# Higher priority for norm and attention steps than for weight splits, and bias tables stored in 16 parts, in a decoder trunk on one core

## The chip, the cores and the metric

The kernel runs on one core of one Trainium2 chip. The metric is device time in microseconds (us); lower is better. The time before is the median of three runs, and one further execution was profiled.

## The reference, cut to what matters

The reference is a decoder trunk of four layers on 256 tokens of width 1024, all in float32. Each layer is a half-step feed-forward (FFN), a token mixer, and a second half-step FFN. Every part is normalised before and after, and added to the residual `x`.

```python
for i in range(DEPTH):                                  # DEPTH = 4
    x = x + 0.5 * rms_norm(swiglu(rms_norm(x, g[0]), w_in[i, 0], w_out[i, 0]), g[1])
    m = mixer[i % 3](rms_norm(x, g[2]))                 # 0: sliding window with sinks, 1: NSA, 2: MoBA
    x = x + rms_norm(m, g[3])
    x = x + 0.5 * rms_norm(swiglu(rms_norm(x, g[4]), w_in[i, 1], w_out[i, 1]), g[5])
```

The mixers have 16 heads of 64 and one bias table by distance, shared by all layers. Layers 0 and 3 use the sliding window of 128, layer 1 uses NSA (compressed blocks, selected blocks and a window), and layer 2 uses full causal blocks.

## The kernel before, in words

**Chains.** The 256 tokens are two tiles of 128, `t` = 0 and 1. Each tile is a chain of steps (`Chain.run`), written as a Python generator that yields the time at which its next step can start. A planner (`choose`, with a `Clock` that books an estimated time for each instruction) interleaves the two chains. The order of TensorE is exactly the order that the planner writes (`ORDERED`). On the other engines a scheduler at compile time orders the instructions: by its own estimate of when an instruction's inputs are there, and among those that are ready on an engine it takes the one with the lowest priority number, which is the place in the written order. At run time each engine takes its instructions in the order so fixed.

**Weights and their splits.** A float32 product is made of three products of a faster kind: a weight is split into `hi` and `lo`, an activation into `xh` and `xl`, and TensorE adds `hi*xh`, `lo*xh` and `hi*xl`. `feed` does the weights: a load of 512 KB (`raw<-wts`, queue SP, 4 buffers), a copy on ScalarE (`hi<-raw`), a subtraction on VectorE (`lo<-raw,hi`). It is called once at each step of the planner's loop, so splits are written ahead of the steps that come after them. Up to 28 slots (`k4`) hold split halves and the attention's tiles, and `room` says how many are left.

**The steps named in the change.**
- `boundary` ends a part: `var` squares the accumulators on ScalarE, `rsqrt` is on GpSimd, the residual `x` is updated on VectorE, then `split_T` transposes the new `x` on TensorE (`trx`) and makes `xh` on ScalarE and `xl` on VectorE. The next part's first products wait for these.
- `core` is the attention core, in jobs of four heads. Scores (`acc<-k,k` in the profile) go to two PSUM banks, VectorE adds the bias and takes the maximum (`k<-acc,bias`), then come the negated maximum (`nm`), the exponentials on ScalarE (`k<-k,nm`), transposes on TensorE (`trp`) copied out to `pT` by both engines, products with the values (`pv`), and the weighing on VectorE (`weigh`). A chain has 4 jobs in layers 0, 2 and 3, and 8 in layer 1.
- In layer 1 two more generators run beside the cores, `compress` and `cmp_core`. Their instructions on ScalarE and VectorE are not touched by the change.
- `setup` builds the bias tables once, early in layer 0: two products, two copies, and four stores to `scratch` in memory (`scratch<-k`), the planner letting `SGAP` = 8 us pass between them. `bias` loads a job's table from there in four parts (`bias<-scratch`).
- `project` multiplies the norm's output with a block of weights in two halves of the 1024 input rows (`proj`); the second half needs `xl[4]` and on.

All queue-SP transfers (weights, tables, biases, gains) are issued in one order. Because of a helper, nearly all instructions have line 210 (ScalarE, VectorE, GpSimd), 228 (products), 235 (transposes) or 248 (transfers) in the profile, so tiles tell them apart.

Of the kernel before, what the change touches and what calls it, by code (L numbers as in the profile page):

```python
# [10 lines left out]
F32 = mybir.dt.float32  # L11
# [32 lines left out]
PACE = 1.2  # L44
LATE = 6
SETUP = 30
SGAP = 8
SOON = 3
HALVES = (slice(0, DH), slice(DH, P))
FIRST, CMP_CORE = -1, 1.5  # L50
# [210 lines left out]
def trunk(ctx: ExitStack, tc: tile.TileContext, x, rel, gains, pre, sinks, pos, w1, w2, wts, hot,  # L261
# [72 lines left out]
    def setup():  # L334
        relx = const.tile([33, 2, H], F32, name="relx")
        hots = k4(3, [P, HALF])[:33, :2 * LT]
        nc.sync.dma_start(relx[0:32], rel)
        nc.vector.memset(relx[32:33], 1.0)
        nc.sync.dma_start(hots, hot)
        nc.sync.dma_start(cm, cmask)  # L340
        nc.sync.dma_start(bm, bmask)
        nc.sync.dma_start(post, pos)
        nc.sync.dma_start(w2s, w2)
        for a in range(2):
            nc.sync.dma_start(nsink[:, a, :], sinks[a:a + 1, :].broadcast_to([P, H]))
        yield when(hots, relx), False
        rows = k4(3, [P, HALF])[:H, :2 * LT].rearrange("p (a b) -> p a b", a=2)
        for i in range(2):
            p = bank([P, 512], "tab")
            nc.tensor.matmul(p[:H, :LT], relx[:, i, :], hots[:, i * LT:(i + 1) * LT],  # L350
                             start=True, stop=True)
            nc.vector.tensor_copy(rows[:, i, :], p[:H, :LT])
        nc.vector.tensor_scalar_mul(nsink, nsink, -1.0)
        for i in (1, 0):
            for c in range(0, REP, REP // 2):
                nc.sync.dma_start(scratch[i, :, c:c + REP // 2],
                                  rows[:, i, :].unsqueeze(1).broadcast_to([H, REP // 2, LT]))
                yield clock.now + SGAP, False
        drop(3, 2)
        plan.want[3] = 0  # L360
# [52 lines left out]
    class Chain:  # L413
# [72 lines left out]
        def boundary(self, acc, this, coef, last=False):  # L486


            t = self.t
            x_ = xt[t]  # L490
            g = self.gain(*this)
            cols = [slice(q * 512, (q + 1) * 512) for q in range(2)]
            r = self.rsqrt(self.var(acc, 1.0 / (coef * coef)))
            ys = []
            for c, a in zip(cols, acc):
                y = k2([P, 512])
                nc.vector.tensor_tensor(y, a, g[:, c], op=ALU.mult)
                ys.append(y)
            accs.extend(acc)
            for c, y in zip(cols, ys):  # L500
                nc.vector.scalar_tensor_tensor(x_[:, c], y, r, x_[:, c], op0=ALU.mult, op1=ALU.add)
                if last:
                    nc.sync.dma_start(out[t * P:(t + 1) * P, c], x_[:, c])
            if last:
                return
            yield max(when(x_), free_bank()), False
            i, k = this
            norm = 6 * i + k + 1
            self.split_T(x_, 0, norm)
            self.split_T(x_, 1, norm)  # L510
            self.v = self.var([x_[:, c] for c in cols], 1.0)
            if t:
                load_gains(((norm + 1) // 6, (norm + 1) % 6))
            yield when(self.xl[0]), True
# [14 lines left out]
        def project(self, n):  # L529
            p = bank([P, 512], "proj")  # L530
            if n > 256:
                self.proj(p, n, 0, 4)
                yield 0.0, True
                self.proj(p, n, 4, 8)
            else:
                self.proj(p, n, 0, 8)
            return p
# [130 lines left out]
        def core(self, o, branches, table, sink=None):  # L668
# [11 lines left out]
            for n in range(len(jobs) + 2):  # L680
                new = None
                if n < len(jobs):
                    h0, br = jobs[n]
                    key = branches[br][0]
                    b0 = h0 // hb * hb
                    if br == 0 and b0 == h0 and b0 + hb < H:
                        biases[b0 + hb] = self.bias(table, b0 + hb)
                    bias = biases[b0][:, h0 - b0:h0 - b0 + 4, :]
                    yield max(free(*sc_), when(self.qT, key(h0))), False
                    for e in range(2):  # L690
                        rows = slice(DH * e, DH * e + DH)
                        for j in range(2):
                            h = h0 + 2 * j + e
                            nc.tensor.matmul(sc[e][:, j, :], self.qT[rows, h // 2, :],
                                             key(h)[rows, :nk], start=True, stop=True)
                    s = k4(t, [P, 4, nk]) if t else k2([P, 4, nk])
                    mx = self.small("mx", 4)
                    for e in range(2):
                        for j in range(2):
                            k = 2 * j + e  # L700
                            nc.vector.tensor_tensor_reduce(
                                s[:, k, :], sc[e][:, j, :], bias[:, k, :], 1.0, -3e38, ALU.add,
                                ALU.max, accum_out=mx[:, k:k + 1])
                    new = (h0, br, s, mx)
                if turned is not None:
                    h0, br, pTs, coef = turned
                    yield max(when(*pTs), free_bank()), False
                    pv = bank([P, 4, DH], "pv")
                    for half in range(2):
                        for c in range(nb):  # L710
                            k, kb = 2 * half + c // (t + 1), c % (t + 1)
                            for q in HALVES:
                                nc.tensor.matmul(pv[q, k, :], pTs[half][:, c, q],
                                                 branches[br][1](h0 + k, kb), share=0.25,
                                                 start=kb == 0, stop=kb == t)
                    self.weigh(o[:, h0 * DH:(h0 + 4) * DH], pv, coef, br == 0)
                done = None
                if fresh is not None:
                    h0, br, s, den, at = fresh
                    pTs = []  # L720
                    for half in range(2):
                        yield max(at[half], free_bank()), False
                        p = bank([P, nb, P], "trp")
                        for c in range(nb):
                            k, kb = 2 * half + c // (t + 1), c % (t + 1)
                            nc.tensor.transpose(p[:, c, :], s[:, k, kb * P:(kb + 1) * P], ident)
                        pT = pp.tile([P, nb, P], F32, tag="pT", name="pT")
                        if half:
                            nc.vector.tensor_copy(pT, p)
                        else:  # L730
                            nc.scalar.activation(pT, p, AF.Copy)
                        pTs.append(pT)
                    if t:
                        drop(t)
                    coef = self.recip(den)
                    gate = branches[br][2]
                    if gate is not None:
                        nc.vector.tensor_tensor(coef, coef, gate[:, h0:h0 + 4], op=ALU.mult)
                    done = (h0, br, pTs, coef)
                    fresh = None  # L740
                if new is not None:
                    h0, br, s, mx = new
                    nm = self.small("nm", 4)
                    if sink is None:
                        nc.vector.tensor_scalar_mul(nm, mx, -1.0)
                    else:
                        ns = nsink[:, sink, h0:h0 + 4]
                        nc.vector.scalar_tensor_tensor(nm, mx, -1.0, ns, op0=ALU.mult, op1=ALU.min)
                    den = self.small("den", 4)
                    at = []  # L750
                    for k in range(4):
                        nc.scalar.activation(s[:, k, :], s[:, k, :], AF.Exp, bias=nm[:, k:k + 1],
                                             accum_out=den[:, k:k + 1])
                        if k % 2:
                            at.append(when(s))
                    if sink is not None:
                        es = self.small("es", 4)
                        nc.vector.tensor_sub(es, nm, ns)
                        nc.scalar.activation(es, es, AF.Exp)
                        nc.vector.tensor_add(den, den, es)  # L760
                    fresh = (h0, br, s, den, at)
                turned = done
            accs.extend(sc_)
# [360 lines left out]
```

## Time and profile before

| | |
|---|---|
| median of three runs | 1981.14 us (1978.83 to 1983.23) |
| profiled execution, its own time | 1981.12 us |
| its span in the profile | 1979.3 us |
| TensorE busy | 1938.0 us, 98% |
| VectorE busy | 1234.2 us, 62% |
| ScalarE busy | 1039.2 us, 53% |
| mean granted TensorE clock | 0.994 |

The span runs from the first to the last instruction; the time has 1.8 us more around it. A busy TensorE is one that has a product under way, so its busy share does not say that it runs at its best rate.

### The profile page before, as it was taken

The numbers are of one execution on the slowest core, as the hardware profiler recorded it, in microseconds if no ns is written. First come the engines' busy times: TensorE is split into PE (matmuls) and PEld (weight loads), VectorE is DVE, ScalarE is ACT, GpSimd is POOL, SyncE is SP. The second block draws the span as 40 slices with busy tenths as digits, with TensorE's granted clock in tenths as the row PEclk, the third lists the DMA queues.
The fourth block names the chain that finished last, engine by engine and source line by source line (L and its number), as shares of the span: only waits on it lengthen the run. The fifth ranks groups of instructions, "written<-read, shape, count | busy, mean of one in ns | idle before, by whom it ended". The sixth has DMA issues, their size and how long they took to land.

```text
span 1979.3 us, 27414 instructions
## 1 busy us (share of the span) xinstructions
PE 1938.0 (98%) x9978; PEld 1586.7 (80%) x9978; DVE 1234.2 (62%) x2267; ACT 1039.2 (53%) x1885; POOL 43.0 (2%) x62
## 2 busy tenths in 40 slices
PE   7999999999999998999999999999999999999998
PEld 6778878888888876788888888778888888878887
DVE  6566666556655648765576556566557655676554
ACT  6345655445544546554455455655445544665442
POOL 0000000000000000000000000000000000000000
PEclk9999999999999999999999999999999999999999
DMA  8758556555556454465556555655555555436551
GB/s 271 210 192 241 176 137 200 190 185 186 195 188 193 153 165 116 139 202 188 185 170 209 185 185 175 188 148 196 185 189 181 195 188 191 161 112 205 185 186 58
DMA packets 114131, 356.42 MB, mean 180 GB/s; under 512 B 12843, under 2 KB 30507, under 8 KB 113996
## 3 DMA queue, kind: packets, MB, share of 16 engines
q1 hardware_dynamic: 113996, 354.68, 55.4%
q8 instruction: 78, 1.28, 0.3%
q14 instruction: 57, 0.47, 0.1%
HBM read 352.01 MB, written 2.62 MB: 179 GB/s over the span
## 4 chain that ended last, share of the span: by engine, by line
PE 90%; ACT 3%; DVE 3%; DMA 2%; issue 1%; SPq 0%; POOL 0%; DVEq 0%; POOLq 0%; ACTq 0%
PE proj L228 56%; PE acc L228 29%; ACT k L210 2%; PE trh L235 2%; DVE k L210 2%; DMA raw<-wts 1%; PE trx L235 1%; DVE lo L210 1%; PE pv L228 1%; DMA bias<-scratch 1%; PE trp L235 1%; ACT hi L210 1%; DVE pT L210 0%; PE trq L235 0%; ACT xh L210 0%
## 5 line engine op out<-in xcount | busy, mean ns | idle before, releaser
L210 DVE TENSOR_TENSOR lo<-raw,hi 128x1024 fp32r<-128x1024 f32 x625 | 760.3, 1223 | 371.3 <-ACT hi L210 338.7
L210 ACT ACTIVATE hi<-raw 128x1024 fp32r<-128x1024 f32 x625 | 659.3, 1063 | 369.3 <-PE acc L228 187.5
L228 PE MATMUL proj<-hi,xh 128*128 128x512 f32 (+1 forms) x1696 | 673.9, 398 | 2.7 <-DVE xl L210 1.7
L228 PE MATMUL proj<-lo,xh 128*128 128x512 f32 (+1 forms) x1696 | 657.4, 389 | 0.8 <-DVE lo L210 0.8
L228 PE MATMUL proj<-hi,xl 128*128 128x512 f32 (+1 forms) x1696 | 448.6, 387 | 0.0
L228 PEld LDWEIGHTS proj<-hi,xh 128*128 128x128 f32 x1696 | 320.0, 189 | 64.0 <-ACT xh L210 2.8
L228 PEld LDWEIGHTS proj<-lo,xh 128*128 128x128 f32 x1696 | 320.4, 189 | 61.4 <-DVE lo L210 1.1
L228 PEld LDWEIGHTS proj<-hi,xl 128*128 128x128 f32 x1696 | 315.6, 188 | 67.3
L228 PE MATMUL acc<-hi,hh 128*128 128x512 f32 x704 | 223.7, 392 | 3.1 <-ACT hh L210 3.1
L228 PE MATMUL acc<-lo,hh 128*128 128x512 f32 x704 | 222.2, 389 | 0.0
L228 PE MATMUL acc<-hi,hl 128*128 128x512 f32 x704 | 191.3, 390 | 0.0
L210 ACT ACTIVATE h<-proj,rh 128x256 f32<-128x256 f32 x176 | 81.9, 465 | 182.3 <-PE proj L228 180.8
L210 ACT ACTIVATE hh<-trh 128x256 fp32r<-128x256 f32 x176 | 67.0, 380 | 180.8 <-PE trh L235 180.7
L228 PEld LDWEIGHTS acc<-hi,hh 128*128 128x128 f32 x704 | 130.9, 188 | 30.2 <-ACT hh L210 3.9
L228 PEld LDWEIGHTS acc<-hi,hl 128*128 128x128 f32 x704 | 132.1, 188 | 27.7
L228 PEld LDWEIGHTS acc<-lo,hh 128*128 128x128 f32 x704 | 132.1, 188 | 27.6
L210 DVE SCALAR_TENSOR_TENSOR h<-h,proj 128x256 f32<-128x256 f32 x176 | 73.6, 418 | 116.2 <-ACT h L210 116.1
L210 DVE TENSOR_TENSOR hl<-trh,hh 128x256 fp32r<-128x256 f32 x176 | 73.9, 420 | 113.2 <-ACT hh L210 113.1
L210 DVE SCALAR_TENSOR_TENSOR h<-proj,c,h 128x256 f32<-128x256 f32 x176 | 85.0, 483 | 5.1
L210 ACT ACTIVATE k<-k,nm 128x128 f32<-128x128 f32 (+1 forms) x160 | 70.7, 445 | 32.0 <-DVE nm L210 32.0
L210 POOL TENSOR_TENSOR r<-v,mhalf 128x1 f32<-128x1 f32 x48 | 36.0, 750 | 1818.4 <-DVE v L210 1818.4
L235 PE MATMUL trh<-ident,h 128*128 128x128 f32 x352 | 67.0, 272 | 0.0
(99 smaller groups left out, 1133.4 us busy)
## 6 DMA issues: line engine op xcount, KB each, us to landing
raw<-wts SPq DMA_DIRECT2D x624, 512.0 KB, 4.6
bias<-scratch SPq DMA_DIRECT2D x96, 128.0 KB, 4.6
g<-gains SPq DMA_DIRECT2D x12, 512.0 KB, 4.8
k<-w SPq DMA_DIRECT2D x8, 512.0 KB, 8.3
scratch<-k SPq DMA_DIRECT2D x4, 384.0 KB, 6.6
out<-x SPq DMA_DIRECT2D x4, 256.0 KB, 2.0
x<-x SPq DMA_DIRECT2D x2, 256.0 KB, 3.0
x<-x SPq DMA_DIRECT2D x1, 512.0 KB, 7.2
```

Of the source, the lines that this page charges most:

```text
L210: return call(out, *args, **kw)
L228: self.engine.matmul(out, lhs, rhs, **kw)
L235: self.engine.transpose(out, src, ident)
```

## The change

1. `SGAP` goes from 8 to 6, and each of the two tables is stored in 8 parts of 4 rows instead of 2 parts of 16: 16 stores instead of 4, of the same bytes in sum.
2. A new constant `AHEAD` = 100. Instructions written inside `tc.high_priority(AHEAD)` get a priority number lower by 100, so among ready instructions of an engine they go before whatever was written up to some 100 instructions earlier. It is put around the post-norm, the residual update, `split_T` and `var` of `boundary`; and in `core` around the bias and maximum, the weighing, the copies `pT`, and the exponentials with `nm` and the sink terms. TensorE's order is written by hand and stays as the planner writes it; `feed`, `out_proj`'s own `split_T`, `compress` and `cmp_core` keep their numbers.
3. `project` yields `when(self.xl[4])` instead of `0.0` between its halves, so that the planner gives the second half no earlier time than that of its input.

```diff
-SGAP = 8
+SGAP = 6
+AHEAD = 100
...
-            for c in range(0, REP, REP // 2):
-                nc.sync.dma_start(scratch[i, :, c:c + REP // 2],
-                                  rows[:, i, :].unsqueeze(1).broadcast_to([H, REP // 2, LT]))
+            for c in range(0, REP, 4):
+                nc.sync.dma_start(scratch[i, :, c:c + 4],
+                                  rows[:, i, :].unsqueeze(1).broadcast_to([H, 4, LT]))
                 yield clock.now + SGAP, False
...
+            with tc.high_priority(AHEAD):
                 r = self.rsqrt(self.var(acc, 1.0 / (coef * coef)))
...
+            with tc.high_priority(AHEAD):
                 self.split_T(x_, 0, norm)
                 self.split_T(x_, 1, norm)
                 self.v = self.var([x_[:, c] for c in cols], 1.0)
...
-                yield 0.0, True
+                yield when(self.xl[4]), True
...
+                    with tc.high_priority(AHEAD):
                         s = k4(t, [P, 4, nk]) if t else k2([P, 4, nk])
                         mx = self.small("mx", 4)
...
+                    with tc.high_priority(AHEAD):
                         self.weigh(o[:, h0 * DH:(h0 + 4) * DH], pv, coef, br == 0)
...
+                        with tc.high_priority(AHEAD):
                             pT = pp.tile([P, nb, P], F32, tag="pT", name="pT")
...
+                    with tc.high_priority(AHEAD):
                         nm = self.small("nm", 4)
```

## Rows read from the trace of the kernel before

**Rows 1.** The page's first part: busy time, share of the span, instructions.
```profile
PE 1938.0 (98%) x9978; PEld 1586.7 (80%) x9978; DVE 1234.2 (62%) x2267; ACT 1039.2 (53%) x1885; POOL 43.0 (2%) x62
```
**Rows 2.** Stretches: length; busy us of PE, PEld, DVE, ACT, POOL; PEclk; DMA.
```profile
100.00:105.00 5.00, 3.64 (x16) 2.46 (x14) 2.54 (x5) 2.76 (x4) 0.00 (x0) 1.00 0.00 0
...
225.00:255.00 30.00, 29.38 (x251) 22.68 (x250) 21.04 (x96) 22.94 (x81) 0.00 (x0) 1.00 0.59 166
255.00:275.00 20.00, 18.02 (x149) 14.96 (x149) 12.57 (x48) 10.51 (x33) 0.55 (x1) 0.96 0.59 127
275.00:660.00 385.00, 385.00 (x1778) 316.84 (x1777) 242.94 (x354) 197.20 (x303) 6.92 (x9) 1.00 0.58 189
...
725.00:803.00 78.00, 67.65 (x806) 51.58 (x805) 67.20 (x275) 47.70 (x165) 6.33 (x8) 0.98 0.45 139
...
1268.00:1313.00 45.00, 41.43 (x385) 33.02 (x385) 30.91 (x124) 32.16 (x102) 0.55 (x1) 1.00 0.55 150
...
1729.00:1773.00 44.00, 40.80 (x344) 31.92 (x342) 30.31 (x127) 28.10 (x96) 0.55 (x1) 0.92 0.38 109
```
**Rows 3.** The chain that ended last, 725 to 806 us: start, us, what.
```profile
732.39 3.50 DVE lo L210 x3
...
762.81 1.13 DVE lo L210
...
798.38 1.11 DVE lo L210
```
**Rows 4.** Timeline of TensorE, 728 to 742 us.
```profile
734.05 1.68 PE L228 MATMUL acc<-k,k 64*128 64x128 f32 x16
```
**Rows 5.** The same chain, 1270 to 1315 us.
```profile
1268.99 1.08 ACT hi L210
...
1271.23 0.59 DVE lo L210
```
**Rows 6.** The same chain, 1720 to 1775 us.
```profile
1733.37 1.23 DVE lo L210
...
1735.47 7.28 DMA bias<-scratch
```
**Rows 7.** Timeline, 264 to 276 us: idle time before it in brackets.
```profile
266.07 1.22 DVE L210 TENSOR_TENSOR lo<-raw,hi 128x1024 fp32r<-128x1024 f32 x1
...
268.14 0.15 DVE L210 SCALAR_TENSOR_TENSOR nm<-mx,nsink 128x4 f32<-128x4 f32 x1
...
273.61 1.94 PE L235 MATMUL trx<-ident,x 128*128 128x128 f32 x8 [1.98 <-DVE x L210]
```
**Rows 8.** Timeline of ScalarE, 75 to 108 us.
```profile
99.49 0.38 ACT L210 ACTIVATE hh<-trh 128x256 fp32r<-128x256 f32 x1 [5.19 <-PE trh L235]
...
102.61 3.89 ACT L210 ACTIVATE hi<-raw 128x1024 fp32r<-128x1024 f32 x4
```
**Rows 9.** The page's transfers: KB each, median us to landing.
```profile
scratch<-k SPq DMA_DIRECT2D x4, 384.0 KB, 6.6
```
**Rows 10.** Groups: count, busy us, mean ns, idle before and releaser.
```profile
L210 DVE TENSOR_TENSOR lo<-raw,hi 128x1024 fp32r<-128x1024 f32 x625 | 760.3, 1223 | 371.3 <-ACT hi L210 338.7 <-PE acc L228 7.6 <-ACT xh L210 2.2
```
**Rows 11.** Waits of TensorE: total us, times, longest.
```profile
PE proj L228 <- DVE xl L210: 1.7, 2, 1.3
PE proj L228 <- DVE lo L210: 0.8, 1, 0.8
```
**Rows 12.** Timelines of VectorE and of TensorE (last row), 486 to 497 us.
```profile
489.29 0.69 DVE L210 TENSOR_TENSOR k<-acc,g 128x512 f32<-128x512 f32 x1
490.03 1.41 DVE L210 SCALAR_TENSOR_TENSOR x<-k,r,x 128x512 f32<-128x512 f32 x2
491.37 1.22 DVE L210 TENSOR_TENSOR lo<-raw,hi 128x1024 fp32r<-128x1024 f32 x1
...
494.77 2.16 DVE L210 SCALAR_TENSOR_TENSOR xl<-trx,pres,xh 128x128 fp32r<-128x128 f32 x8 [0.77 <-ACT xh L210]
...
495.21 0.39 PE L228 MATMUL proj<-lo,xh 128*128 128x512 f32 x1
```

More of the change, by code (lines that the diff above doesn't have):

```diff
@@ L492, in boundary @@
             cols = [slice(q * 512, (q + 1) * 512) for q in range(2)]
[L493 to L503, printed above, removed]
+            with tc.high_priority(AHEAD):
+                r = self.rsqrt(self.var(acc, 1.0 / (coef * coef)))
+                ys = []
+                for c, a in zip(cols, acc):
+                    y = k2([P, 512])
+                    nc.vector.tensor_tensor(y, a, g[:, c], op=ALU.mult)
+                    ys.append(y)
+                accs.extend(acc)
+                for c, y in zip(cols, ys):
+                    nc.vector.scalar_tensor_tensor(x_[:, c], y, r, x_[:, c], op0=ALU.mult, op1=ALU.add)
+                    if last:
+                        nc.sync.dma_start(out[t * P:(t + 1) * P, c], x_[:, c])
             if last:
@@ L508, in boundary @@
             norm = 6 * i + k + 1
-            self.split_T(x_, 0, norm)
-            self.split_T(x_, 1, norm)
-            self.v = self.var([x_[:, c] for c in cols], 1.0)
+            with tc.high_priority(AHEAD):
+                self.split_T(x_, 0, norm)
+                self.split_T(x_, 1, norm)
+                self.v = self.var([x_[:, c] for c in cols], 1.0)
             if t:
@@ L695, in core @@
                                              key(h)[rows, :nk], start=True, stop=True)
[L696 to L703, printed above, removed]
+                    with tc.high_priority(AHEAD):
+                        s = k4(t, [P, 4, nk]) if t else k2([P, 4, nk])
+                        mx = self.small("mx", 4)
+                        for e in range(2):
+                            for j in range(2):
+                                k = 2 * j + e
+                                nc.vector.tensor_tensor_reduce(
+                                    s[:, k, :], sc[e][:, j, :], bias[:, k, :], 1.0, -3e38, ALU.add,
+                                    ALU.max, accum_out=mx[:, k:k + 1])
                     new = (h0, br, s, mx)
@@ L715, in core @@
                                                  start=kb == 0, stop=kb == t)
-                    self.weigh(o[:, h0 * DH:(h0 + 4) * DH], pv, coef, br == 0)
+                    with tc.high_priority(AHEAD):
+                        self.weigh(o[:, h0 * DH:(h0 + 4) * DH], pv, coef, br == 0)
                 done = None
@@ L726, in core @@
                             nc.tensor.transpose(p[:, c, :], s[:, k, kb * P:(kb + 1) * P], ident)
[L727 to L731, printed above, removed]
+                        with tc.high_priority(AHEAD):
+                            pT = pp.tile([P, nb, P], F32, tag="pT", name="pT")
+                            if half:
+                                nc.vector.tensor_copy(pT, p)
+                            else:
+                                nc.scalar.activation(pT, p, AF.Copy)
                         pTs.append(pT)
@@ L742, in core @@
                     h0, br, s, mx = new
[L743 to L760, printed above, removed]
+                    with tc.high_priority(AHEAD):
+                        nm = self.small("nm", 4)
+                        if sink is None:
+                            nc.vector.tensor_scalar_mul(nm, mx, -1.0)
+                        else:
+                            ns = nsink[:, sink, h0:h0 + 4]
+                            nc.vector.scalar_tensor_tensor(nm, mx, -1.0, ns, op0=ALU.mult, op1=ALU.min)
+                        den = self.small("den", 4)
+                        at = []
+                        for k in range(4):
+                            nc.scalar.activation(s[:, k, :], s[:, k, :], AF.Exp, bias=nm[:, k:k + 1],
+                                                 accum_out=den[:, k:k + 1])
+                            if k % 2:
+                                at.append(when(s))
+                        if sink is not None:
+                            es = self.small("es", 4)
+                            nc.vector.tensor_sub(es, nm, ns)
+                            nc.scalar.activation(es, es, AF.Exp)
+                            nc.vector.tensor_add(den, den, es)
                     fresh = (h0, br, s, den, at)
```

## The prediction

> **What bounds the kernel now.** I read the page's first part, then busy time by stretch, then the chain that ended last, and then timelines at the places where TensorE stood idle. TensorE is busy for 98% of the span [rows 1]. VectorE and ScalarE have room in the mean, so work that moves between places on them costs nothing unless TensorE waits for it. The stretches say where it does. From 275 to 660 us, two FFNs with the norms between them, TensorE is busy for 385.00 of 385 us [rows 2]: there the priority can only hide what is hidden already. Its idle time stands in five places: 5.00 - 3.64 = 1.4 us in the setup of layer 0, 2.0 us at the end of layer 0's attention (255 to 275), 10.4 us in layer 1's cores (725 to 803), 3.6 us in layer 2's (1268 to 1313) and 3.2 us in layer 3's (1729 to 1773) [rows 2]. That is 20.6 us, 1% of the time, and it is the most that the change can win back, beside what the clock gives. The first stretch of layer 0's cores (225 to 255) has only 0.6 us of it.
>
> In the cores the reader should see a chain that goes round VectorE, ScalarE and TensorE, in which now and then a weight split stands. One `lo` takes 1223 ns in the mean [rows 10], about as long as the whole bias-and-maximum step of a small job, so one split ahead of a step that is due delays the chain by up to 1.2 us.
>
> **The change part by part.** The terms are worked out against the profiled execution's own time, 1981.12 us (span 1979.3 and 1.8 around it); the median of the runs is 1981.14, so the two are the same for this purpose.
>
> *The setup.* ScalarE is idle for 5.19 us before an FFN step at 99.49, and the copies `hi` that TensorE needs come four in a row at 102.61, all behind the FFN steps [rows 8]: the order fixed at compile time held them to be late, behind the stores to `scratch`, of which each lands in 6.6 us [rows 9]. TensorE waits 1.4 us for these splits. With parts of a quarter of the size, the weight loads between them are held up for a quarter as long each, and the splits spread out. I take the whole 1.4 us. Bounds: 0, and a loss: if every one of 16 stores brought a quarter of that stall, they would cost 16 x 0.34 = 5.4 us instead of 1.4. I take the gain, since the run makes 625 splits [rows 10] in 1979 us, one load of 512 KB every 3.2 us, and a store of 96 KB is small beside that. The 12 added issues on SP are hidden by its waits for free buffers. The two slots of `k4` stay taken longer (16 x 6 = 96 us instead of 32), which makes the lead of the splits one half shorter in the first FFN; no cost taken.
>
> *Layer 0, end of the attention.* Right behind the last maximum a split of 1.22 us starts at 266.07, and `nm` only at 268.14; the exponentials follow, then the squares of the other chain's norm behind them on ScalarE, and TensorE waits 1.98 us for `x` at 273.61 [rows 7]. With priority the split goes behind. The weighing and the copy `pT` that also stand there have the same priority and stay. I take 1.0 us; bounds 0 and 2.0 [rows 2].
>
> *Layer 1.* Splits stand on the chain for 3.50, 1.13 and 1.11 us, in sum 5.7 [rows 3]. Not all of the 3.50 is to be had: the scores that VectorE needs next are made from 734.05 to 735.7 [rows 4], so before about 734.9 the splits filled a gap, and only 1.0 us of them was in the way. That leaves 1.0 + 1.1 + 1.1 = 3.2 us. A split that has begun is not broken off, so a step that comes at any moment still waits for part of one; I take two thirds, 2.2 us. Bounds 0 and 5.7. VectorE is busy for 67.2 of these 78 us [rows 2], so what helps here is that splits move out of the stretch, not that they swap places in it.
>
> *Layers 2 and 3.* In layer 2, a `hi` of 1.08 and a `lo` of 0.59 us stand on the chain as the cores begin, 1.7 in sum [rows 5]; I take 1.0, bounds 0 and 3.6. In layer 3, a split of 1.23 us stands ahead of the steps that free a bias buffer, and the load of the next bias, 7.28 us until it is there, starts only after them [rows 6]. Moving the split aside starts that load earlier by as much; I take 0.9, bounds 0 and 3.2. The load itself is late next, and it keeps the rest of the idle time.
>
> *The FFN boundaries.* The norm steps pass splits and the other chain's FFN steps there. TensorE has no idle time to win [rows 2], so I count nothing. The cover is the lead of the splits: only once in the whole run does a product wait for a `lo`, 0.8 us [rows 11], and that is the setup's stall. I charge as much, 0.8 us, for splits that come late in the new order.
>
> *The planner's time for the second half.* Only layers 1 and 2 begin with a block wider than 256, so four places change. TensorE waits for `xl` at products 1.7 us in sum, two times [rows 11]; that is the most to be won, and a chain put back by one block could lose as much. I take 0.
>
> Sum: 1.4 + 1.0 + 2.2 + 1.0 + 0.9 - 0.8 = 5.7 us less, 1981.1 - 5.7 = 1975.4 us.
>
> *The clock.* In three of the stretches with idle time the granted clock is below one in the mean: 0.96, 0.98 and 0.92 [rows 2]. The levels are 2.4 and 1.2 GHz, so in layer 3 TensorE ran for 2 x 0.08 x 44 = 7 us at the lower one. What that could give back at most is 0.04 x 20 + 0.02 x 78 + 0.08 x 44 = 5.9 us, if nothing else held TensorE then. Nothing in the rows says that a shorter idle time lifts it, so I keep it for the range.
>
> **The rivals.**
>
> *More than the sum.* Every split on the chains goes aside in full, and idle time behind it closes: 1.4 + 2.0 + 5.7 + 3.6 + 3.2 = 15.9 us, 1965.2 us, further if the clock stays up. For it: the idle times are there. Against it: the chains of layers 1 to 3 consist of much else, among it the 7.28 us bias load. Chance 0.10, for 9 us and more.
>
> *The priority changes nothing where it counts.* It moves an instruction only past others that are ready at the same moment by the compile-time estimate. Where the estimate has the split run before the step is ready, the order stays, and TensorE's idle time is the latency of the chain itself. Many splits also run in gaps in which VectorE has nothing else to do: it sat idle for 338.7 us in sum before a `lo`, waiting for its `hi` [rows 10]. Then only the setup gains: 1981.1 - 1.4 = 1979.7 us. Chance 0.31, with cases where gains and losses cancel.
>
> *Splits come too late (the other side).* After each norm of the second chain an FFN begins with little lead. At 491.37 a `lo` runs that ends at 492.6 and is used at 495.21: 2.6 us of slack, with a product by the gain (`k<-acc,g`, 0.69 us, one of two) and `x` (1.41 us) just before it and `xl` (2.16 us) after it [rows 12]. This pattern stands at seven FFN starts. If the new order puts a split behind `x`, both products by the gain and `xl`, some 4.9 us, TensorE waits 4.9 - 2.6 = 2.3 us at each, 16 us in all: 1975.4 + 16 = 1991 us. It eats up the forecast gain from a wait of 0.8 us at each place on, that is from a delay of 3.4 us. For it: 100 places in the written order are several steps of the planner. Against it: `xl` is ready only at 494.77, after the split, and a split that is ready does not wait for a step that is not. Chance 0.14.
>
> A rule of the Trainium skill speaks for this rival (TensorE: Matmul & The Clock Gate, section on the architectural detail of the array): ScalarE and VectorE take their queues strictly in order, so a privileged step whose input comes later than estimated holds up every split behind it. The trace agrees so far as VectorE sat idle before a `lo` until its `hi` came, 338.7 us in sum [rows 10], and ran nothing from behind it. By the rule alone the time would go toward this rival's 1991 us; by the rows, where it is the splits that are waited for and not the core steps, it stays at the sum.
>
> **How the numbers follow.** The forecast, 4 to 9 us less, has 0.45; the larger gain 0.10; no effect 0.31; late splits 0.14. About 0.2% of the time, 4.0 us, is what a measurement of this kernel can tell from no change: faster means under 1977.2, slower over 1985.1. So faster has 0.45 + 0.10 = 0.55, same 0.31, slower 0.14. The range goes from 1967 (the larger gain almost whole) to 1983 (no effect, with the setup's loss of about 2 us), and leaves out the late splits and a tail below, under 0.2 together. Given that the forecast is right in kind, its own range is 1972 to 1977.
>
> **What would show it right or wrong.** Right: TensorE idle from 102 to 105 is gone; at the end of layer 0's attention `nm` follows the last maximum at once; in layers 1 to 3 fewer `lo` and `hi` stand on the chain, the bias load in layer 3 is issued about a microsecond earlier, and FFN stretches keep a full TensorE. Wrong: products that wait for `lo` or `hi` at FFN starts; the same splits in the same places on the chain; or `compress` and `cmp_core`, which keep their numbers, holding TensorE longer in layer 1 because core steps pass them on VectorE.

## The result, and the profile after

| | before | after |
|---|---|---|
| median, same chip | 1981.21 us (1978.83 to 1983.23) | 2014.14 us (2013.17 to 2020.31) |
| ratio, 95% interval | | 1.0174 [1.0157, 1.019] |
| span of the profiled execution | 1979.3 us | 2012.9 us |
| mean granted TensorE clock | 0.994 | 0.987 |

The change makes the kernel 33 us slower. I had forecast 1975.4 us with a range up to 1983. The first part of the page after answers to [rows 1]: every engine does the same number of instructions.

```profile
PE 1949.6 (97%) x9978; PEld 1595.8 (79%) x9978; DVE 1235.2 (61%) x2267; ACT 1041.3 (52%) x1885; POOL 33.4 (2%) x62
```

TensorE is busy 11.6 us more in a span that is 33.6 us longer. So some 22 us are new idle time, and some 12 us are products that take longer. TensorE's waits after name the idle time (total us, times, longest):

```profile
PE trh L236 <- DVE h L211: 19.7, 7, 3.1
PE trx L236 <- DMA x<-x: 9.0, 2, 5.4
PE acc L229 <- DVE mx L211: 6.9, 7, 1.7
PE trc L236 <- DVE k L211: 4.7, 2, 3.9
PE trx L236 <- DVE x L211: 2.7, 3, 2.0
...
PE hidT L236 <- DVE k L211: 1.8, 1, 1.8
...
PE proj L229 <- DVE xl L211: 1.7, 2, 1.3
```

The first row is new: before, no transpose of `h`, the FFN's hidden tile, waited for VectorE. There are seven such waits, one for each FFN but the last. `trc` belongs to `cmp_core` in layer 1 and waited 1.8 us before. No row names `lo` or `hi`: no product waits for a split.

One of the seven places, in timelines of ScalarE, VectorE and TensorE after, stands for all (the other six have the same order, `xl` ahead of `h`; the first has no split between the two `h`, and its wait is the shortest, 1.9 us). Chain 0 is at the norm behind its FFN, and chain 1 is still in its own:

```profile
473.36 2.16 ACT L211 ACTIVATE xh<-trx,pres 128x128 fp32r<-128x128 f32 x8
475.36 0.53 ACT L211 ACTIVATE h<-proj,rh 128x256 f32<-128x256 f32 x1
```

```profile
474.87 0.15 DVE L211 TENSOR_SCALAR rh<-r 128x1 f32<-128x1 f32 x1 [0.73 <-POOL r L211]
474.94 2.15 DVE L211 SCALAR_TENSOR_TENSOR xl<-trx,pres,xh 128x128 fp32r<-128x128 f32 x8
477.00 0.41 DVE L211 SCALAR_TENSOR_TENSOR h<-h,proj 128x256 f32<-128x256 f32 x1
477.33 1.22 DVE L211 TENSOR_TENSOR lo<-raw,hi 128x1024 fp32r<-128x1024 f32 x1
478.47 0.48 DVE L211 SCALAR_TENSOR_TENSOR h<-proj,c,h 128x256 f32<-128x256 f32 x1
```

```profile
474.92 1.07 PE L229 MATMUL acc<-hi,hl 128*128 128x512 f32 x4
479.10 0.41 PE L236 MATMUL trh<-ident,h 128*128 128x128 f32 x2 [3.11 <-DVE h L211]
```

At the same place before, the two products `h` came ahead of `xl`, and the transpose did not wait (VectorE, then TensorE):

```profile
471.35 0.41 DVE L210 SCALAR_TENSOR_TENSOR h<-h,proj 128x256 f32<-128x256 f32 x1
...
471.80 0.48 DVE L210 SCALAR_TENSOR_TENSOR h<-proj,c,h 128x256 f32<-128x256 f32 x1
...
473.37 2.15 DVE L210 SCALAR_TENSOR_TENSOR xl<-trx,pres,xh 128x128 fp32r<-128x128 f32 x8
```

```profile
473.37 0.38 PE L235 MATMUL trh<-ident,h 128*128 128x128 f32 x2
```

What the raised `xh` and `xl` passed is the tanh and the products of the other chain's FFN, which TensorE needs next by its written order. The slack of `h` was 473.37 - 472.28 = 1.1 us; `xl` alone takes 2.15. ScalarE was done with the tanh at 475.89, and VectorE was free for `h` only when `xl` ended, at 477.09, so here `xl` holds `h` up longer than `xh` does.

The Trainium skill (TensorE: Matmul & The Clock Gate, section on the architectural detail of the array) says that VectorE takes its queue strictly in order. The trace agrees: the second `h` has the first behind it at 477.41 and starts at 478.47, after the `lo` that the order put between them.

The products that take longer stand behind these waits. Stretches after, with the columns of [rows 2]:

```profile
200.00:205.00 5.00, 3.09 (x18) 2.53 (x17) 3.46 (x12) 1.70 (x6) 0.20 (x1) 0.94 0.95 228
205.00:210.00 5.00, 5.00 (x26) 4.66 (x25) 0.06 (x1) 1.67 (x4) 0.00 (x0) 0.71 0.17 35
...
476.00:486.00 10.00, 6.90 (x32) 5.75 (x33) 6.04 (x13) 3.58 (x5) 0.00 (x0) 1.00 0.57 191
...
669.00:674.00 5.00, 4.90 (x17) 4.02 (x18) 0.42 (x1) 0.39 (x1) 0.00 (x0) 0.69 0.33 108
...
1030.00:1035.00 5.00, 4.55 (x14) 3.73 (x15) 2.97 (x5) 0.46 (x2) 0.00 (x0) 0.66 0.64 197
...
1222.00:1230.00 8.00, 7.54 (x22) 6.05 (x23) 1.87 (x3) 0.39 (x1) 0.00 (x0) 0.60 0.40 133
...
1539.00:1544.00 5.00, 4.83 (x16) 3.97 (x17) 2.69 (x5) 0.39 (x1) 0.00 (x0) 0.66 0.71 230
...
1731.00:1736.00 5.00, 4.55 (x33) 4.32 (x34) 0.73 (x2) 1.55 (x4) 0.00 (x0) 1.00 0.33 105
```

Behind five of the seven waits the granted clock is 0.60 to 0.71 in the mean, so part of these stretches ran at 1.2 GHz; behind the two that end at 479 and 1731 it stayed at 2.4. What that costs is (1 - clock) x length: 1.45 + 1.55 + 1.7 + 3.2 + 1.7 = 9.6 us. Waits and lost work make 19.7 + 9.6 = 29.3 us, close to the 28.4 us by which the seven stages grow in the table below.

TensorE's order is the same before and after but for two swaps of twelve products in layer 0, so the start of the same product in both traces says where time went. The table gives what the difference, after minus before, grows by in each stage (stages by their time before, us):

| the seven boundaries | | the rest | |
|---|---|---|---|
| 199 to 225 | +3.2 | setup, up to 107 | -2.0 |
| 470 to 496 | +3.4 | layer 0's cores, 225 to 281 | +0.6 |
| 655 to 690 | +3.8 | layer 1's cores, 750 to 775 | +6.4 |
| 1008 to 1035 | +4.4 | layer 1's cores, 775 to 806 | -1.3 |
| 1195 to 1222 | +5.8 | layer 2's cores, 1222 to 1320 | +1.0 |
| 1505 to 1535 | +4.7 | all else | +0.4 |
| 1693 to 1725 | +3.1 | | |
| sum | +28.4 | sum | +5.1 |

The table compares two single executions. Its -1.3 between 775 and 806 stands with -1.2 in the trace of `e1_setup_only` as well, where nothing is raised: the granted clock of this stretch was 0.94 in the trace of before and 1.00 there, so it is not the priority's.

### The profile page after: what moved, and what is told of

Its sections match the earlier page's. It is cut to its first block, busy times and chain, and to the rows that moved or that the text cites. A ratio compares the mean times of both kernels' runs of the same rounds, so it can differ in the third digit from the quotient of the medians.

```text
span 2012.9 us, 27459 instructions
## 1 busy us (share of the span) xinstructions
PE 1949.6 (97%) x9978; PEld 1595.8 (79%) x9978; DVE 1235.2 (61%) x2267; ACT 1041.3 (52%) x1885; POOL 33.4 (2%) x62
## 4 chain that ended last, share of the span: by engine, by line
PE 85%; DVE 5%; ACT 4%; DMA 3%; issue 1%; POOL 0%; SPq 0%; DVEq 0%; POOLq 0%; ACTq 0%
PE proj L229 53%; PE acc L229 27%; DMA raw<-wts 3%; ACT k L211 2%; PE trh L236 2%; DVE lo L211 2%; DVE k L211 1%; ACT hi L211 1%; PE pv L229 1%; PE trx L236 1%; PE trp L236 1%; ACT junk L211 1%; DVE xl L211 1%; DMA bias<-scratch 1%; ACT xh L211 0%
## 5 line engine op out<-in xcount | busy, mean ns | idle before, releaser
L236 PE MATMUL trh<-ident,h 128*128 128x128 f32 x352 | 68.3, 276 | 19.9 <-DVE h L211 19.7
L236 PEld LDWEIGHTS trh<-ident,h 128*128 128x128 f32 x352 | 48.3, 140 | 44.4 <-issue 22.5
```

Of the source, the lines that this page charges most:

```text
L236: self.engine.transpose(out, src, ident)
```

## The experiments

The theories. **A**: raised norm steps hold up the other chain's FFN steps. **B**: splits come too late (the prediction's rival on the slow side). **C**: the setup with its 16 stores costs the time. **D**: raised core steps pass `compress` and `cmp_core`. Every kernel is the one before with the edit named; each ratio is to runs of the kernel before on the same chip.

### One part of the change at a time

`e1_setup_only`: part 1 of the change alone.

```diff
-SGAP = 8
+SGAP = 6
...
-            for c in range(0, REP, REP // 2):
+            for c in range(0, REP, 4):
```

> Only the 16 smaller stores and the gap of 6 us of the change; no priorities, the planner's time between the halves as before. Theory A (the loss is that privileged norm steps hold up the other chain's FFN steps): the stall at 102 to 105 us is gone, 2 to 3 us less than before, about 1978.5 us. Theory B (privileged steps make the splits late, the rival of the prediction) expects the same here. Theory C (the loss comes with the setup: its smaller stores or the slots it holds longer): 10 to 33 us more than before.

Measured: 1980.75 us, 0.9997 [0.9986, 1.0007]. In its trace the setup wins its 2 us, as in the table above, and layer 3 gives 2.2 us back, at a granted clock of 0.88 where it was 0.92 [rows 2]. In the runs together neither shows, though 2 to 3 us were expected. C falls.

`e2_norm_only`: the two raised blocks of `boundary` alone.

```diff
+            with tc.high_priority(AHEAD):
                 r = self.rsqrt(self.var(acc, 1.0 / (coef * coef)))
...
+            with tc.high_priority(AHEAD):
                 self.split_T(x_, 0, norm)
```

> Of the change only the priority on the norm steps; setup, planner's time and attention cores as before. Theory A: all seven waits of the first chain's norms are there, each about 3 us of TensorE idle before a transpose of h, and the clock falls after some of them: 27 to 32 us more than before, about 2011 us. Theory B: products that wait for lo or hi, and a smaller part of the loss, since the core steps are not privileged. Theory D (the core steps pass compress and cmp_core, whose numbers stay): little, under 5 us more than before.

Measured: 2011.24 us, 1.0155 [1.0129, 1.018]. Its waits of TensorE have nearly the same row as after:

```profile
PE trh L236 <- DVE h L211: 19.2, 7, 3.1
...
PE trh L236 <- DVE r L211: 2.5, 1, 2.5
```

Six of the seven in the first row are at the boundaries, and the seventh boundary, that of layer 0, is the second row; the wait left over in the first row, 1.2 us at 840, is the one told of at `e8_mixer_norms`.

`e3_core_only`: the four raised blocks of `core` alone.

```diff
+                    with tc.high_priority(AHEAD):
                         s = k4(t, [P, 4, nk]) if t else k2([P, 4, nk])
...
+                    with tc.high_priority(AHEAD):
                         nm = self.small("nm", 4)
```

> Of the change only the priority on the steps of the attention core; setup, planner's time and norms as before. Theory A: no wait for h at FFN boundaries; layer 1 longer by 3 to 5 us, the other layers unchanged within 1 us each: 1981 to 1986 us. Theory D: most of the 33 us, about 2010 us. The prediction's own view of the cores would be 5 us less than before, 1976 us.

Measured: 1991.71 us, 1.0054 [1.004, 1.0069]. No transpose of `h` waits here. The core steps, which were to win time, lose 11 us, 6.5 of it between 750 and 775. Timelines of VectorE and of TensorE there:

```profile
768.53 2.35 DVE L211 TENSOR_TENSOR lo<-raw,hi 128x1024 fp32r<-128x1024 f32 x2
770.80 0.42 DVE L211 CUSTOM_DVE_ANT_0 k<-acc,bias 128x256 f32<-128x256 f32 x1
...
772.72 0.42 DVE L211 TENSOR_TENSOR k<-scc,cm 128x256 f32<-128x256 f32 x1
...
774.72 0.42 DVE L211 CUSTOM_DVE_ANT_0 k<-acc,bias 128x256 f32<-128x256 f32 x1 [0.25 <-PE acc L229]
...
776.44 0.41 DVE L211 TENSOR_REDUCE nmc<-k 128x16 f32<-128x256 f32 x1
...
778.39 0.43 DVE L211 TENSOR_TENSOR k<-k,cm 128x256 f32<-128x256 f32 x1 [0.48 <-ACT k L211]
```

```profile
778.96 0.41 PE L236 MATMUL trc<-ident,k 128*128 128x128 f32 x2 [3.90 <-DVE k L211]
```

The steps of `cmp_core` (`k<-scc,cm`, `nmc`, `k<-k,cm`) stand behind two rounds of core steps, and TensorE, whose order is fixed, waits 3.90 us for their result. Before, the same transpose waited 1.79 us:

```profile
772.37 0.41 PE L235 MATMUL trc<-ident,k 128*128 128x128 f32 x2 [1.79 <-DVE k L210]
```

Neither theory had this size: A's range ended at 1986 us, and D, whose mechanism this is, had put most of the 33 us here.

### Theory A against its rivals

`e4_ffn_steps_too`: the whole change, with the FFN's own steps raised as well, so that norm steps can't pass them.

```diff
+                with tc.high_priority(AHEAD):
                     nc.scalar.activation(h, p[:, :FB], AF.Tanh, scale=rh)
...
+                with tc.high_priority(AHEAD):
                     nc.scalar.activation(hh, tr, AF.Copy)
```

> The whole change, and in addition the same priority on the FFN's own steps on ScalarE and VectorE (tanh, the two h products, hh, hl). Theory A: the norm steps no longer pass them, so the waits for h go back to nothing and about 30 us come back: 1981 to 1986 us. Theory B: the splits are passed by still more steps, so the time stays at 2014 us or grows.

Measured: 1989.12 us, 1.0034 [1.0021, 1.0047]; `trh` waits for `h` twice, 3.8 us in sum, neither time at one of the seven boundaries (2.5 us at 58, 1.3 us at 842). Of the 32.9 us, 8.7 are left, though splits are passed by still more steps than after. That is 3 us above A's range, which had left out the core's loss: in this trace 6.5 us lie between 750 and 775 again. So A holds for the boundaries, and B falls.

`e5_norm_first_block` and `e6_norm_second_block`: `e2_norm_only` taken apart, only the post-norm and the residual raised, or only the transposes, `xh`, `xl` and `var`.

```diff
# e5_norm_first_block
+            with tc.high_priority(AHEAD):
                 r = self.rsqrt(self.var(acc, 1.0 / (coef * coef)))
# e6_norm_second_block
+            with tc.high_priority(AHEAD):
                 self.split_T(x_, 0, norm)
```

> Before, with the higher priority on the first half of the boundary alone (the post-norm with its products by the gain, and the residual update). Theory A (the seven waits at the FFN boundaries come from the splits of the new x, 8 x xh on ScalarE and 8 x xl on VectorE, that pass the other chain's FFN steps): this half holds the other chain up by no more than the 1.4 us of the two residual updates, so the time stays within 3 us of 1981, and transposes of h wait for VectorE's h for less than 4 us in sum. Rival (every privileged norm step takes its share): VectorE spends about as long on this half, 2 x 0.69 and 1.41 us, as on the xl, so some 40% of the loss of the norm steps alone appears here, about 1993 us.

> Before, with the higher priority on the second half of the boundary alone (transposes of the new x, xh, xl, and the squares of var). Theory A: nearly the whole loss of the norm steps is here, 2006 to 2012 us, with seven waits of about 2.7 us at transposes of h and the lower granted clock behind most of them. Rival (both halves share it): about 1998 us.

Measured: first block 1978.16 us, 0.9989 [0.9978, 1.0]; second block 2010.2 us, 1.0153 [1.0132, 1.0174]. The loss is that of the second block, as A has it; `xh`, `xl` and the squares of `var` in it were not run apart. The residual update, which VectorE does in 1.4 us, costs nothing; its gain of 2 to 3 us is at the edge of what can be told.

`e8_mixer_norms`: part 1 of the change, and `boundary`'s blocks raised only where a mixer ends.

```diff
+            with (tc.high_priority(AHEAD) if k == 3 else nullcontext()):
                 self.split_T(x_, 0, norm)
```

> The stores in 16 parts with SGAP 6, and the higher priority on the boundary only where the norm ends a mixer; nothing on the core and nothing on the norms that end an FFN. Theory A: at these four norms the other chain is still in its attention and not in an FFN, so no transpose of h waits, the setup's 2 us are won and up to 1 us at each layer's end, 1975 to 1980 us. Rival (a privileged norm step costs whatever the other chain is doing): 4 of 11 such norms, so a third of the norm steps' loss, about 1990 us.

Measured: 1978.75 us, 0.9989 [0.9976, 1.0003]. In the median the same raised steps cost nothing where the other chain isn't in an FFN. One transpose of `h` did wait, 1.2 us at 828, where the expectation had none: the tanh stands there behind a `hi` that had waited 2.35 us for its weights, and `h` behind the `lo` of it, not behind a norm step.

`e12_whole_but_one_block`: the whole change with the line of `e8_mixer_norms` in place of its own, the first block raised everywhere.

> The whole change, with one part undone: the second half of the boundary (transposes, xh, xl, var) keeps its higher priority only where the norm ends a mixer. Theory A: the seven waits go and with them 19.7 us of waiting and about 10 us of lower granted clock behind them, so what is left is the core's loss of some 10 us less the setup's 2: 1985 to 1991 us. Rival (the parts' losses overlap and something else in the whole change holds TensorE too, since the norm steps alone lost 30 us, the core's alone 11, and both with the setup 33 and not 39): 1994 us or more.

Measured: 1988.59 us, 1.0049 [1.003, 1.0067]. Undoing this one block at the norms that end an FFN leaves 8.0 us of the 32.9, and most of what is left is the loss of the core steps (6.4 us again between 750 and 775, with the 3.9 us at `trc`).

### What the core steps pass, and what passing splits is worth

`e7_core_and_compress`: `e3_core_only`, with the ScalarE and VectorE steps of `compress` and `cmp_core` raised too (`up` puts each call inside `tc.high_priority(AHEAD)`).

```diff
-            nc.vector.tensor_reduce(nm, s, axis=mybir.AxisListType.X, op=ALU.max, negate=True)
+            up.vector.tensor_reduce(nm, s, axis=mybir.AxisListType.X, op=ALU.max, negate=True)
...
```

> Before, with the higher priority on the attention core as in the run of the core's steps alone, and on all ScalarE and VectorE steps of compress and cmp_core as well, so that neither passes the other. Theory D (the core's loss in layer 1 comes from core steps passing compress and cmp_core on VectorE, for which TensorE then waits): the 6.5 us between 750 and 775 come back, 1983 to 1986 us, and no transpose trc waits 3.9 us. Rival (the core steps lose by passing splits, or by the order among themselves): it stays at 1990 to 1993 us.

Measured: 1985.53 us, 1.002 [1.001, 1.003]. The difference at 775 goes from +7.5 to -0.6 us, and the 3.9 us at `trc` is gone: D holds for layer 1. The rest, 4.5 us in the medians, lies by its trace in layers 2 and 3 (+1.7 and +2.3 us). In layer 3 the trace of `e1_setup_only`, where nothing is raised, grows by 2.2 us as well, so that part is not told from scatter; the cause of the other stays open.

`e9_splits_behind`: nothing raised, the splits lowered.

```diff
+            with tc.high_priority(-BEHIND):          # BEHIND = 30
                 nc.scalar.activation(hi[:, :n], r[:, :n], AF.Copy)
                 nc.vector.tensor_tensor(lo[:, :n], r[:, :n], hi[:, :n].bitcast(F32), op=ALU.subtract)
```

> Before, with nothing raised: instead the two instructions of a split (hi on ScalarE, lo on VectorE) get a priority number higher by 30, so that any other step which is ready may pass splits written up to 30 instructions earlier, and no step of a norm or core passes a step of the other chain's FFN or of compress. Theories A and D (the loss comes from passing steps that are not splits): no loss at the FFN boundaries and none in layer 1, so 1978 to 1984 us, and no transpose of h waits for VectorE for more than 1 us. Rival (late splits cost): products wait for lo or hi at FFN starts, 1985 to 1995 us. If passing splits has a value of its own, as my forecast had it, the time is about 1977 us.

Measured: 1983.88 us, 1.0015 [1.0004, 1.0027]. This is the change's own idea without its side effects, though with a reach of 30 and not 100, and it wins nothing; the interval lies just above 1. The stretches say why (compare [rows 2]):

```profile
725.00:803.00 78.00, 67.18 (x812) 50.80 (x811) 67.15 (x274) 49.49 (x168) 6.23 (x8) 1.00 0.50 146
1268.00:1313.00 45.00, 41.44 (x382) 33.01 (x382) 31.00 (x124) 32.14 (x102) 0.55 (x1) 1.00 0.54 147
1729.00:1773.00 44.00, 39.98 (x305) 31.33 (x305) 26.68 (x120) 25.47 (x90) 0.00 (x0) 0.84 0.41 109
```

TensorE's idle time in the cores is 10.8, 3.6 and 4.0 us, against 10.4, 3.6 and 3.2 before. And the splits stand on the chain that ended last as they did in [rows 3] and [rows 5] (start, us, what; layer 1, then layer 2):

```profile
734.18 3.50 DVE lo L211 x3
762.90 0.49 DVE lo L211
763.95 0.39 DVE lo L211
765.50 1.13 DVE lo L211
798.99 1.11 DVE lo L211
```

```profile
1269.10 1.08 ACT hi L211
...
1271.34 0.59 DVE lo L211
```

Nor does a reach of 100 move them: in `e7_core_and_compress`, whose core steps may pass splits and hold up nothing of `cmp_core`, 3.40, 1.13 and 1.11 us of `lo` stand on the chain of layer 1, with a further 1.12 us at 761.

One part of the expectation failed: a transpose of `h` waits 2.73 us, at 56 in the first FFN. The product that the tanh reads had ended at 48.1, but on ScalarE the tanh stands behind a `hi` that waited 1.74 us for its weights, and runs only at 52.94; on VectorE one `lo` stands ahead of the first `h` and one between the two. So even with its number raised by 30 a split was put ahead of a step whose product was there first when the kernel ran.

### The dose

`e10_ahead_10`: the whole change, with one number smaller.

```diff
-AHEAD = 100
+AHEAD = 10
```

> The whole change with AHEAD = 10 in place of 100. In the compile-time order, the tanh of the other chain's FFN stands before the xh again at the boundaries of layer 0, as in the kernel before, while many splits are still passed. Theory A: most of the seven waits are gone, and of their 30 us at least 20 come back, so 1983 to 1994 us, the rest being the core's loss in layer 1 and what is left at boundaries where the two steps stand closer than 10 instructions. Rival (what a norm step loses hangs on the raised priority itself and not on what it passes): 2005 to 2014 us.

Measured: 1980.76 us, 0.9993 [0.9977, 1.0009]. All the loss is gone, the core's too, and my expectation kept too much of it. ScalarE's timeline, at the place shown above:

```profile
472.45 0.45 ACT L211 ACTIVATE h<-proj,rh 128x256 f32<-128x256 f32 x1
472.81 0.87 ACT L211 ACTIVATE xh<-trx,pres 128x128 fp32r<-128x128 f32 x3
```

The tanh is ahead of `xh` again, and no transpose of `h` waits in the whole run. So it is not the raised priority itself that costs the time, but a reach of 100 places in the written order, which takes in the other chain's steps.

### The parts that cost nothing, together

`e11_first_blocks_and_mixer`: `e8_mixer_norms` with the first block raised everywhere.

> The parts that cost nothing, together: stores in 16 parts with SGAP 6, the higher priority on the first half of every boundary (post-norm and residual), and on the second half (transposes, xh, xl, var) only where a mixer's norm ends; nothing on the core. Theory A: no transpose of h waits, so the gains of the setup (2 us), of the first half (2 us) and of the mixer norms (1 us) may add up to 1975 to 1978 us. Rival (those gains are one and the same clock stretch or are lost in what follows): 1979 to 1981 us, no different from before.

Measured: 1980.08 us, 0.9993 [0.9979, 1.0007]. Its profiled execution is 5.4 us shorter in span than that of before, with a clock of 0.998; the runs together show no difference. No version tried beats the kernel before by more than the measurement can tell.

## Why the prediction was wrong

**The failed step** is that of the FFN boundaries: "TensorE has no idle time to win [rows 2], so I count nothing. The cover is the lead of the splits". No idle time bounds the gain, not the loss. I had written that norm steps pass the other chain's FFN steps there, and then named a cover for the splits alone. What such a passing costs could be had from the trace of before: 2.15 us of `xl` and a `lo` of 1.22 against a slack of 1.1 us, so 2.3 us at each of seven places, 16 us. Measured: 19.7 us of waits, and 9.6 us of lower granted clock behind five of them; undone alone, all but 8.0 of the 32.9 us come back. The 0.8 us that I did charge there, for late splits, came to nothing.

**The setup** was right in kind: from 100 to 105 us TensorE is busy for all 5.00 us, and the stage wins 2.0 us where I had 1.4. In the median of whole runs it does not show. Whether the smaller parts or the shorter gap does it was not run apart.

**Layer 0's end and layers 1 to 3** had 5.1 us of gains; there is none. (That they hold all of TensorE's idle time was misread too: of 1979.3 - 1938.0 = 41.3 us the five places have 20.6, and 11.4 lie in the first 50 us, which the change leaves as they are.) In layer 0 a `lo` still stands behind the last maximum and ahead of `nm`, as in [rows 7] (VectorE after):

```profile
267.60 1.22 DVE L211 TENSOR_TENSOR lo<-raw,hi 128x1024 fp32r<-128x1024 f32 x1
...
269.67 0.15 DVE L211 SCALAR_TENSOR_TENSOR nm<-mx,nsink 128x4 f32<-128x4 f32 x1
```

In layer 3, 2.35 and 1.13 us of `lo` stand ahead of the bias load where one of 1.23 stood [rows 6] (the chain that ended last, after):

```profile
1764.49 2.35 DVE lo L211 x2
...
1768.09 1.13 DVE lo L211
...
1769.63 7.12 DMA bias<-scratch
```

In `e9_splits_behind` splits were put 30 places back, and stand in these places still. That is the rival "the priority changes nothing where it counts", to which I gave 0.31: where the split runs, the estimate at compile time has no step ready that could go first. That this estimate is the reason was argued from the order; the estimate itself was not measured.

**Layer 1** went the other way, by the mechanism that stands last in the prediction as a sign of being wrong: core steps pass `compress` and `cmp_core`. I named it and gave it no price; 6.5 us is its measure in `e3_core_only`.

**The rival of late splits** had the right sign and the wrong cause. No product waits for `lo` or `hi` after. The in-order rule cited there was right too, for another step: what is held up behind a privileged step is not a split but the other chain's `h`.

**The planner's time for `xl[4]`**: 0, as taken; the waits for `xl` are 1.7 us, two times, before and after [rows 11]. It was not run alone.

**The parts don't add up exactly**: 30.8 (norm) + 11.3 (core) - 2 (setup in its stage) is 40, and the whole loses 33. In the traces each of the two parts alone loses a further 2.3 and 2.6 us between 1745 and 1775, which the whole does not. That goes with the clock and not with the priority: `e1_setup_only`, where nothing is raised, loses 2.2 us there too, at a granted clock of 0.93 in this stretch, where it was 1.00 before. The rest of the difference stays open.

## What to carry to other kernels

Raising a priority is a statement about everything that it passes, not only about what it is meant to pass: list what lies within its reach on each in-order engine, and take the slack of each from the trace. Where TensorE is busy throughout, there is no idle time to win, and a delay beyond a step's slack is a loss. A split or other filler on the critical chain is no proof that a lower priority would move it: first find out whether the step behind it was ready when it started.

## What was not expected of the hardware

A wait of about 3 us costs half as much again: 19.7 us of waits were followed by 9.6 us of work lost at 1.2 GHz. Not each wait is: that of 3.11 us which ends at 479 left the granted clock at 1.00, and at the first boundary, where TensorE is busy for 3.09 us of the 5 from 200 to 205, a mean of 0.71 followed. Nor does the place decide: in `e2_norm_only` a wait of 3.1 us that ends at 478 was followed by 0.73, and one of 3.1 us that ends at 1022 by 1.00, the other way round from after (1.00 behind 479, 0.66 behind 1030):

```profile
478.00:484.00 6.00, 5.71 (x20) 4.70 (x21) 2.81 (x5) 0.38 (x1) 0.00 (x0) 0.73 0.73 233
...
1022.00:1028.00 6.00, 6.00 (x28) 4.95 (x27) 2.34 (x4) 0.63 (x2) 0.00 (x0) 1.00 0.76 245
```

What decides between them stays open.

The scatter of runs of one kernel follows the granted clock. The runs of `e10_ahead_10` go from 1975.57 us at 0.996 to 1983.57 us at 0.992; 0.004 x 1980 = 7.9 us, about the whole difference of 8.0 (a clock is given to 0.001, which is 2 us here). A gain of 2 us in one stage can't be told in such medians.
